# An output projection and a gate by seven products instead of eight, in a phase of their own

## The chip, the cores and the metric

The kernel runs on one core of one Trainium2 chip. The metric is the device time of one execution in microseconds; lower is better. All operands are float32. A matmul of float32 precision is made of three matmuls of a rounded type (float32r): each operand is split into a high half (the rounded value) and a low half (the rest), and high x high, low x high and high x low are added up in PSUM.

## The reference

A decoder trunk of two layers on 2048 tokens of 1024 features. Layer A is an mLSTM, layer B a dilated window attention. After each of them a gated embedding is added. What the change touches is the end of layer A:

```python
y = ht.reshape(Bsz, S, A_VW) * jax.nn.silu(z)          # 2048 x 1024
h = x + y @ w_out                                       # w_out 1024 x 1024
gate = jax.nn.sigmoid(rms_norm(h, norm_g) @ w_gate)     # w_gate 1024 x 1024
h = h + (p_l @ w_proj) * gate                           # p_l 2048 x 256
```

Layer B then reads h: it projects keys, values, queries and a gate from it, and adds to it.

## The kernel before, in words

Tokens go in NG = 4 groups of T = 512. Features lie on the 128 partitions, so an activation of one group is KD = 8 tiles of 128 x 512. A group passes through all of layer A and the projections of layer B before the next one starts: `a_in(g)` (mLSTM), `a_out(g)` (output projection and gate), `b_in(g)` (projections of layer B, written to DRAM). For the last group `b_in` runs beside the attention, whose small units are handed out one at a time by `pump()` between the steps of a projection.

`project` is the projection of everything: for each of the 8 slices of the contraction it loads a weight piece of 128 x 512 (`weights`: a DMA from SyncE's queue into `wraw`, then `split`: ScalarE writes the high half `wh`, VectorE subtracts it to get the low half `wl`), and makes 4 x 3 matmuls with 512 columns into 4 PSUM banks. There are 8 banks of 2 KB a partition in all, so one projection accumulates while the one before is read. The lines 145 and 147 are the matmuls with features and with tokens on the output's partitions.

In `a_out`, `mix_out` (L243) adds the banks to the residual x in SBUF, splits h times the norm's weight into the operands of the gate, and adds up its squares (`squares`: ScalarE squares, GpSimd adds, L184). `ple` multiplies the gate's banks by 1/rms of each token (`rstd_hooks`: a product with ones, GpSimd's power, a row spread by a product with a diagonal, L216), takes tanh, and multiplies by the embedding projection (`w_p`, contraction 256). `done` splits the new h for layer B, adds up squares, and writes it to DRAM (`h2d`, L519) for the residual of layer B. The mLSTM's result y is transposed on TensorE inside the output projection (`turn`), and goes from PSUM straight into operands.

The order of the instructions on each engine is written by a scheduler when the kernel is built, from program order and priorities: `tc.high_priority(offset=...)` moves what is in it ahead by so many places. On the chip each engine, and SyncE's DMA queue, runs its list in order and waits by semaphores. Tiles come from pools: a tag has a fixed number of buffers, and a new tile waits until the buffer's last reader is done.

Of the kernel before, what the change touches and what calls it, by code (L numbers as in the profile page):

```python
# [8 lines left out]
F32 = mybir.dt.float32  # L9
# [5 lines left out]
P = 128  # L15
SEQ = 2048
DM = 1024
T = 512
# [23 lines left out]
def trunk_kernel(ctx: ExitStack, tc: tile.TileContext, I: dict, O: dict, upto: int = 9):  # L42
# [6 lines left out]
    wp = ctx.enter_context(tc.tile_pool(name="wp", bufs=1))  # L49
    xp = ctx.enter_context(tc.tile_pool(name="xp", bufs=12))  # L50
    tm = ctx.enter_context(tc.tile_pool(name="tm", bufs=2))
    sm = ctx.enter_context(tc.tile_pool(name="sm", bufs=2))

# [28 lines left out]
    def scratch(name, shape):  # L82
        return O[name] if name in O else dram.tile(shape, F32, name=name)

    h2d = scratch("h2d", [NG, KD, P, T])
    kd = scratch("kd", [SEQ, 512])
# [82 lines left out]
    def sumsq(dst, src):  # L169
        jk = sm.tile([P, 512], BF16, name="jk", tag="jk", bufs=1)  # L170
        n = src.shape[-1]
        nc.scalar.activation(jk[:, :n], src, AF.Square, accum_out=dst)  # L172

    def pj(n=512):
        return sm.tile([P, n], F32, name="pj", tag="pj", bufs=8)

    def squares(acc, k, src, eng=nc.gpsimd):
        """acc += src**2 (acc = src**2 for k = 0)."""
        if k == 0:
            nc.scalar.activation(acc, src, AF.Square)  # L180
        else:
            sq = sm.tile([P, T], F32, name="sq", tag="sq", bufs=2)
            nc.scalar.activation(sq, src, AF.Square)  # L183
            eng.tensor_tensor(acc, acc, sq, op=ALU.add)  # L184

    def new_acc():
        return sm.tile([P, T], F32, name="acc", tag="acc", bufs=2)

    def token_rstd(acc):
# [4 lines left out]
        r = sm.tile([P, NT], F32, name="rst", tag="rst", bufs=4)  # L194
        rsqrt(r, ps[:, 0:NT], 1.0 / DM, NT)
        return r

    def spread(rst):
        """Diagonals of rst, [P, NT, P], in two parts."""
        rh = sm.tile([P, NT], F32R, name="rh", tag="rh", bufs=2)  # L200
        rl = sm.tile([P, NT], F32, name="rl", tag="rl", bufs=2)
        nc.vector.tensor_copy(rh, rst)
        nc.vector.tensor_tensor(rl, rst, rh.bitcast(F32), op=ALU.subtract)
        parts = []
        for r in (rh.bitcast(F32), rl):
            dg = sm.tile([P, NT, P], F32R, name="dg", tag="sq", bufs=2)
            nc.vector.tensor_tensor(dg, ident.unsqueeze(1).broadcast_to([P, NT, P]),
                                    r.unsqueeze(2).broadcast_to([P, NT, P]), op=ALU.mult)
            parts.append(dg)
        return parts  # L210

    def row_rstd(parts):
        """The same along the free axis on every partition: [P, T]."""
        ps = bank()
        for j, dg in enumerate(parts):
            nc.tensor.matmul(ps, onesr, dg.rearrange("p t s -> p (t s)"), start=j == 0, stop=j == 1)  # L216
        rb = sm.tile([P, T], F32, name="rb", tag="rb", bufs=1)
        nc.scalar.copy(rb, ps)
        return rb
# [8 lines left out]
    def tok(g):  # L228
        return slice(g * T, (g + 1) * T)

    def mix_out(src, nk, X, res, l, order=None, hooks={}):
        """h = res + X @ w (features on partitions), the operands of the gate and the sum of squares."""
        h = tm.tile([P, KD, T], F32, name="h", tag="v", bufs=1)
        for k in range(KD):
            nc.sync.dma_start(h[:, k], res[k])
        sq = new_acc()
        X2 = []
        for grp in range(2):
            acc = project(src[grp], 512, nk, X, True, order=order, hooks=hooks if grp == 0 else {})
            with tc.high_priority(offset=EVAC):  # L240
                for i in range(NT):
                    k = grp * NT + i
                    nc.vector.tensor_tensor(h[:, k], acc[i], h[:, k], op=ALU.add)  # L243
# [42 lines left out]
    def a_in(g):  # L286
# [13 lines left out]
        hooks = rstd_hooks(st, sq, *((R3, R4) if g else (5, 7)))  # L300
# [79 lines left out]
        Y = {}  # L380

        def turn(*ks):
            transposed([z[:, t] for t in range(NT)], ks, gam[:, G_H], Y)

# [4 lines left out]
        return Y, turn  # L389
# [24 lines left out]
    def mlstm_pre(pre, qk, t, n, ga):  # L414
        """What chunk n needs that does not depend on the state; ga: [P, 8] its gates."""
# [93 lines left out]
    def a_out(g, X, turn):  # L509
        hooks = {s: lambda k=k: turn(*k) for s, k in HO.items()}  # L510
        h, X, sq = mix_out(I["w_out_a"], 8, X, I["xT"][g], 0, (0, 1, 6, 7, 2, 3, 4, 5), hooks)
        sq2 = new_acc()
        X2 = []

        def done(k, hk):
            X2.append(new_x())
            split(*X2[k], hk, 1.0)
            squares(sq2, k, hk)
            nc.sync.dma_start(h2d[g, k], hk)  # L519

        ple(0, g, h, X, sq, done)
        return X2, sq2

    def rope_table(g, t, which):
        """[P, 2, 2, 64]: (g1 cos, g2 cos), (-g2 sin, g1 sin)."""
        n = g * NT + t
        cst = sm.tile([P, P], F32, name="cst", tag="cst", bufs=2)
        nc.sync.dma_start(cst, I["cs"][n * P:(n + 1) * P, :])
        tab = sm.tile([P, 2, 2, 64], F32, name="tab", tag=f"tab{which}", bufs=NT)
# [8 lines left out]
    def b_in(g, X, sq, late=lambda: None):  # L538
# [27 lines left out]
        st = {}  # L566
        acc = project(I["w_kv"][0], 512, 8, X, False, gam[:, G_KV], hooks={5: lambda: st.update(r=token_rstd(sq))})
        rst = st["r"]
# [39 lines left out]
    bp = ctx.enter_context(tc.tile_pool(name="bp", bufs=2))  # L608
# [17 lines left out]
    def attend(grp, r, res, b, kv, prev, finish, mdtag="md"):  # L626
        """One block of 128 queries of a head group with its own keys and those of the block before."""
# [159 lines left out]

    held = [[] for _ in range(NT)]
# [7 lines left out]
    b_in(NG - 1, X, sq, lambda: side.append(staged(first[-NL:] + tailed())))  # L796
# [25 lines left out]
def layout(inputs):  # L822
# [13 lines left out]

    wa = f["w_in_a"][0]
# [5 lines left out]
    d["w_out_a"] = pieces(f["w_out_a"][0], 512)  # L843
# [39 lines left out]
```

## Time and profile before

| | us |
|---|---|
| median of three runs | 2370.97 (2367.55 to 2373.04) |
| span of the profiled execution | 2372.5 |
| TensorE (PE) busy | 2318.8 (98%) |
| VectorE (DVE) busy | 1553.0 (65%) |
| ScalarE (ACT) busy | 1132.0 (48%) |
| GpSimd (POOL) busy | 605.1 (26%) |
| DMA | 330.86 MB, mean 139 GB/s |
| one `a_out` of 512 tokens (window 216.5 to 319) | 102.5 |

The profile is of one execution; its span is 1.5 us above the median of the runs. PEld is the loading of weights into TensorE, beside the matmuls. A line of the groups reads: source line, engine, operation, output tile <- input tiles, shapes, count, then busy time, mean duration in ns, idle time of the engine just before it and who ended that. An answer for one line of the source gives minimum, median and maximum of the durations instead. In a table of windows each engine has its busy time and number of instructions in that stretch.

### The profile page before, as it was taken

Reading aid. Unit: us, or ns where it says so; the run is one execution under the profiler, and the core shown is the slowest. Engines: PE = TensorE matmul, PEld = TensorE weight load, DVE = VectorE, ACT = ScalarE, POOL = GpSimd, SP = SyncE. Lnnn points to the kernel's source line nnn. Section 1 sums busy time; section 2 is a strip of 40 time slices with the busy share of each in tenths; the row PEclk is TensorE's granted clock in tenths of the full one; section 3 lists DMA queues with packets and bytes.
Section 4 is the critical chain, followed back from the end, with each engine's and each line's share of the span. In section 5 each row is a group of like instructions: output and inputs, shape, how many; then the busy total and the mean of one; then the engine's idle time right before and its main releaser. Section 6 shows DMA issues by size and latency. Waiting matters only on the chain.

```text
span 2372.5 us, 35281 instructions
## 1 busy us (share of the span) xinstructions
PE 2318.8 (98%) x11736; PEld 1976.7 (83%) x11736; DVE 1553.0 (65%) x3405; ACT 1132.0 (48%) x2730; POOL 605.1 (26%) x719
## 2 busy tenths in 40 slices
PE   8999999899999999999999999999999998999998
PEld 7889888788988887889888788888898887888887
DVE  7746675675567566746674676476754667786865
ACT  5334444543344454434444543344664665453643
POOL 5020244701212464011225710212112121220311
PEclk9999999999999999999999999999999999999999
DMA  5323334533234444323344443254563776464452
GB/s 157 125 75 121 111 122 158 164 101 120 66 125 124 149 137 142 118 90 114 99 129 152 145 125 120 66 165 124 196 222 126 233 239 217 145 195 159 146 164 94
DMA packets 186791, 330.86 MB, mean 139 GB/s; under 512 B 21168, under 2 KB 37872, under 8 KB 186608
## 3 DMA queue, kind: packets, MB, share of 16 engines
q1 hardware_dynamic: 186608, 328.59, 43.5%
q8 instruction: 93, 1.52, 0.3%
q14 instruction: 90, 0.74, 0.1%
HBM read 277.98 MB, written 50.53 MB: 138 GB/s over the span
## 4 chain that ended last, share of the span: by engine, by line
PE 84%; DVE 5%; POOL 4%; DMA 3%; issue 2%; ACT 1%; SPq 0%; DVEq 0%; POOLq 0%; ACTq 0%
PE bank L147 40%; PE bank L145 32%; PE bank L683 2%; PE bank L652 2%; PE bank L621 1%; PE bank L483 1%; PE bank L485 1%; PE bank L482 1%; POOL acc L184 1%; PE bank L160 1%; PE bank L672 1%; POOL rq L560 1%; DMA oo<-o2d 1%; PE bank L469 1%; DVE y L735 1%
## 5 line engine op out<-in xcount | busy, mean ns | idle before, releaser
L147 PE MATMUL bank<-wh,xh 128*128 128x512 f32 (+1 forms) x1664 | 641.4, 385 | 0.0
L147 PE MATMUL bank<-wh,xl 128*128 128x512 f32 (+1 forms) x1664 | 621.8, 374 | 0.0
L147 PE MATMUL bank<-wl,xh 128*128 128x512 f32 (+1 forms) x1664 | 621.0, 373 | 0.0
L95 ACT ACTIVATE wh<-wraw 128x512 fp32r<-128x512 f32 (+1 forms) x544 | 327.3, 603 | 579.8 <-PE bank L145 301.7
L97 DVE TENSOR_TENSOR wl<-wraw,wh 128x512 fp32r<-128x512 f32 (+1 forms) x512 | 361.1, 709 | 314.3 <-ACT wh L95 312.5
L145 PE MATMUL bank<-xh,wh 128*128 128x512 f32 x1280 | 508.9, 398 | 14.7 <-ACT wh L95 13.8
L145 PE MATMUL bank<-xh,wl 128*128 128x512 f32 x1280 | 503.4, 393 | 1.8 <-DVE wl L97 1.8
L145 PE MATMUL bank<-xl,wh 128*128 128x512 f32 x1280 | 501.7, 392 | 0.0
L147 PEld LDWEIGHTS bank<-wh,xl 128*128 128x128 f32 x1664 | 312.7, 188 | 50.5
L147 PEld LDWEIGHTS bank<-wh,xh 128*128 128x128 f32 x1664 | 313.1, 188 | 48.1
L147 PEld LDWEIGHTS bank<-wl,xh 128*128 128x128 f32 x1664 | 313.3, 188 | 47.7
L184 POOL TENSOR_TENSOR acc<-acc,sq 128x512 f32<-128x512 f32 x105 | 164.2, 1564 | 543.1 <-ACT sq L183 540.2
L145 PEld LDWEIGHTS bank<-xh,wh 128*128 128x128 f32 x1280 | 242.5, 190 | 65.1 <-ACT wh L95 15.0
L145 PEld LDWEIGHTS bank<-xh,wl 128*128 128x128 f32 x1280 | 243.2, 190 | 51.9 <-DVE wl L97 3.6
L145 PEld LDWEIGHTS bank<-xl,wh 128*128 128x128 f32 x1280 | 242.7, 190 | 51.5
L99 DVE SCALAR_TENSOR_TENSOR wl<-wraw,gam,wh 128x512 fp32r<-128x512 f32 x192 | 159.4, 830 | 156.4 <-ACT wh L95 155.2
L95 ACT ACTIVATE wh<-wraw,gam 128x512 fp32r<-128x512 f32 x192 | 138.4, 723 | 220.0 <-PE bank L147 166.2
L664 ACT ACTIVATE pr<-pr,nm 128x256 f32<-128x256 f32 (+1 forms) x192 | 86.5, 453 | 43.8 <-DVE nm L661 43.6
L558 POOL TENSOR_SCALAR ssb<-ssb,r 128x4 f32<-128x4 f32 x64 | 27.5, 430 | 257.0 <-ACT jk L172 235.5
L652 PE MATMUL bank<-kT,qT 128*128 128x128 f32 x600 | 79.2, 280 | 7.3 <-DVE pT L676 3.7
L652 PEld LDWEIGHTS bank<-kT,qT 128*128 128x128 f32 x600 | 73.8, 194 | 10.6 <-DVE pT L676 5.2
L560 POOL TENSOR_TENSOR rq<-ssb,mhalf 128x4 f32<-128x4 f32 x64 | 77.7, 1214 | 5.3
(402 smaller groups left out, 2943.6 us busy)
## 6 DMA issues: line engine op xcount, KB each, us to landing
wraw<-in_w_pg SPq DMA_DIRECT2D x128, 256.0 KB, 2.7
wraw<-in_w_in_b SPq DMA_DIRECT2D x128, 256.0 KB, 2.7
wraw<-in_w_z SPq DMA_DIRECT2D x96, 172.0 KB, 2.3
wraw<-in_w_v SPq DMA_DIRECT2D x64, 256.0 KB, 2.6
wraw<-in_w_o SPq DMA_DIRECT2D x64, 256.0 KB, 2.6
wraw<-in_w_out_a SPq DMA_DIRECT2D x64, 256.0 KB, 2.6
wraw<-in_w_kv SPq DMA_DIRECT2D x64, 256.0 KB, 2.7
kr<-kd SPq DMA_DIRECT2D x53, 256.0 KB, 4.0
```

Source lines behind the costliest of these rows:

```text
L95: nc.scalar.mul(dst_h, src, scale)
L97: nc.vector.tensor_tensor(dst_l, src, dst_h.bitcast(F32), op=ALU.subtract)
L99: nc.vector.scalar_tensor_tensor(dst_l, src, scale, dst_h.bitcast(F32), op0=ALU.mult, op1=ALU.subtract)
L145: nc.tensor.matmul(acc[i], w[:, cs], x, start=first, stop=last)
L147: nc.tensor.matmul(acc[i][:, :n], x[:, cs], w, start=first, stop=last)
L160: nc.tensor.transpose(tp[:, t * P:(t + 1) * P], tiles[t][:, k * P:(k + 1) * P], ident)
L184: eng.tensor_tensor(acc, acc, sq, op=ALU.add)
L558: nc.gpsimd.tensor_scalar(ss, ss, r2[:, t:t + 1], EPS, op0=ALU.mult, op1=ALU.add)
L560: nc.gpsimd.tensor_tensor(rq, ss, mhalf, op=ALU.pow)
L652: nc.tensor.matmul(sp[:, hh * n + j * P:hh * n + (j + 1) * P], qT[:, hs], kvs[j]["k"][:, hs], start=True, stop=True)
L664: nc.scalar.activation(pr[:, hh, :n], pr[:, hh, :n], AF.Exp, bias=nm[:, h:h + 1], accum_out=md[:, 4 + h:5 + h])
L683: nc.tensor.matmul(op[:, hs], pTs[h // 2][:, c0 + j * P:c0 + (j + 1) * P], kvs[j]["v"][:, hs], start=j == 0, stop=j == nk - 1)
```

## The change

Output projection and gate leave the loop over groups. The program has three phases now. The first runs `a_in` for all groups and writes y (transposed and scaled) to DRAM (`yd`), then the embedding projections of all groups (`ple_parts`, result in `pwd`). The second is new: four stages (output of tokens 0 to 1023, of 1024 to 2047, gate of the same two), each by Strassen's algorithm in its variant of Winograd. The 1024 tokens, the contraction and a block of 512 output columns are halved, and seven products of 512 tokens x 512 x 256 take the place of eight. Their operands are quarters of X and W or sums of such, split into halves after the sum; some results are carried on in PSUM (`chain`), some copied to SBUF and added there. Output goes to DRAM (`h1d`, then `h2d`). The third phase is layer B, which loads h from `h2d` and splits it. SBUF is laid out anew for each phase, in the same place; a tile of the new phase waits only for those tiles whose place it takes.

The products of a stage run in the order PR for each of two column blocks (nb). The operands of the next product's weights are made one product ahead; the seven operands of X of the next stage during the last column block of the stage before it.

```diff
-    for g in range(NG - 1):
-        b_in(g, *a_out(g, *a_in(g)))
-    X, sq = a_out(NG - 1, *a_in(NG - 1))
-    pa.close()
+    late = {}
+    for g in range(NG):
+        turn = a_in(g, late)
+        late = {s: lambda k=k, turn=turn: turn(*k) for s, k in HO.items()}
+    rest = list(late.values())
+    for g in range(NG):
+        ple_parts(g, ...)
+    pa.close()
+    p1.close()
...
         def turn(*ks):
-            transposed([z[:, t] for t in range(NT)], ks, gam[:, G_H], Y)
+            for k in ks:
+                tp = bank()
+                for t in range(NT):
+                    nc.tensor.transpose(tp[:, t * P:(t + 1) * P], z[:, t, k * P:(k + 1) * P], ident)
+                b = pj()
+                nc.scalar.mul(b, tp, gam[:, G_H, k:k + 1])
+                nc.sync.dma_start(yd[g, k], b)
...
+    PR = (1, 2, 6, 5, 7, 3, 4)
+    def sub(out, a, b, eng):
+        eng.tensor_tensor(out, a, b, op=ALU.subtract)
+    def halves(hi, lo, t):
+        nc.scalar.copy(hi, t)
+        nc.vector.tensor_tensor(lo, t, hi.bitcast(F32), op=ALU.subtract)
+    def x_operand(st, p):
+        hi = xs.tile([P, 4, T], F32R, name=f"xh{p}", tag=f"xh{p}")
+        lo = xs.tile([P, 4, T], F32R, name=f"xl{p}", tag=f"xl{p}")
+        st.X[p] = (hi, lo)
+        for kh in range(2):
+            ks = slice(2 * kh, 2 * kh + 2)
+            def ld(h, kq):
+                t = so.tile([P, 2, T], F32, name="xr", tag="xr", bufs=5)
+                k0 = 4 * kq + 2 * kh
+                nc.sync.dma_start(t, st.src[2 * st.s + h, k0:k0 + 2].rearrange("k p t -> p k t"))
+                return t
...
+            elif p == 6:
+                t, u, v = ld(1, 0), ld(1, 1), ld(0, 0)
+                nc.gpsimd.tensor_tensor(t, t, u, op=ALU.add)
+                sub(t, t, v, nc.vector)
+            elif p == 5:
+                t, u = ld(1, 0), ld(1, 1)
+                nc.gpsimd.tensor_tensor(t, t, u, op=ALU.add)
+            elif p == 7:
+                t, u = ld(0, 0), ld(1, 0)
+                sub(t, t, u, nc.gpsimd)
+            else:
+                t = ld(0, 1)
+                sub(t, t, st.X[6][0][:, ks].bitcast(F32), nc.vector)
+                sub(t, t, st.X[6][1][:, ks].bitcast(F32), nc.vector)
+            halves(hi[:, ks], lo[:, ks], t)
+    def w_load(st, nb):
+        B = {}
+        for kq, nq in ((0, 0), (1, 0), (0, 1), (1, 1)):
+            t = so.tile([P, 4, 256], F32, name="wr", tag="wr", bufs=5)
+            nc.sync.dma_start(t, st.w[nb, kq, nq].rearrange("p (k c) -> p k c", k=4))
+            if st.g is not None:
+                for k in range(4):
+                    nc.vector.tensor_scalar(t[:, k], t[:, k], gam[:, st.g, ...], None, op0=ALU.mult)
+            B[kq, nq] = t
+        return B
+    def w_operand(B, p):
...
+        elif p == 6:
+            t1 = B[0, 0]
+            sub(t1, B[0, 1], t1, nc.gpsimd)
+            t = B["t2"] = so.tile([P, 4, 256], F32, name="t2", tag="t2", bufs=1)
+            sub(t, B[1, 1], t1, nc.vector)
...
+        elif p == 7:
+            t = B[0, 1]
+            sub(t, B[1, 1], t, nc.gpsimd)
...
+        else:
+            t = B[1, 0]
+            sub(t, t, B["t2"], nc.gpsimd)
+        hi = so.tile([P, 4, 256], F32R, name="sh", tag="sh", bufs=2)
+        lo = so.tile([P, 4, 256], F32R, name="sl", tag="sl", bufs=2)
+        halves(hi, lo, t)
+    def multiply(st, p, w, banks, first, last):
+        for f in range(2):
+            for k in range(4):
+                for j, (a, b) in enumerate(((wh, xh), (wl, xh), (wh, xl))):
+                    nc.tensor.matmul(banks[f], a[:, k, cs], b[:, k], ...)
+    def run_stages(stages, hooks):
...
+        for p in PR:
+            x_operand(stages[0], p)
+            if p == 1:
+                fetch(0)
+        for n, (i, nb, p) in enumerate(flat):
+            with tc.high_priority(offset=60):
+                fetch(n + 1)
...
+            multiply(st, p, ops.pop(n), dst, p in (1, 2, 5), p in (4, 2, 3))
+            if nb == st.nbs - 1 and i + 1 < len(stages):
+                with tc.high_priority(offset=60):
+                    x_operand(stages[i + 1], p)
+            with tc.high_priority(offset=EVAC):
+                for j in range(2):
+                    if p in (1, 6, 5):
+                        parts[p, j] = st.first(h, f, dst[j])
+                    else:
+                        part = {2: 1, 7: 5, 3: 6, 4: None}[p]
+                        st.final(h, f, dst[j], parts.pop((part, j)) if part else None)
+    def gather(accs, h, v):
...
+            nc.scalar.activation(sqt, v, AF.Square)
+            nc.gpsimd.tensor_tensor(accs[h], accs[h], sqt, op=ALU.add)
+    def out_stage(s, accs):
+        def first(h, f, acc):
+            t = residual(h, f)
+            nc.vector.tensor_tensor(t, acc, t, op=ALU.add)
+            return t
+        def final(h, f, acc, t):
+            if t is None:
+                t = residual(h, f)
+            nc.vector.tensor_tensor(t, acc, t, op=ALU.add)
+            nc.sync.dma_start(h1d[2 * s + h, f], t)
+            gather(accs, h, t)
+    def ple_stage(s, rbs, accs):
+        def first(h, f, acc):
+            t = stile()
+            nc.scalar.copy(t, acc)
+            return t
+        def final(h, f, acc, t):
+            hh, pw = (so.tile([P, T], F32, name=n, tag=n, bufs=2) for n in ("hh", "pw"))
+            nc.sync.dma_start(hh, h1d[2 * s + h, f])
+            nc.sync.dma_start(pw, pwd[2 * s + h, f])
+            if t is None:
+                t = stile()
+                nc.vector.tensor_tensor(t, acc, rbs[h], op=ALU.mult)
+            else:
+                nc.vector.tensor_tensor(t, acc, t, op=ALU.add)
+                nc.gpsimd.tensor_tensor(t, t, rbs[h], op=ALU.mult)
+            nc.scalar.activation(t, t, AF.Tanh, scale=0.5)
+            nc.vector.scalar_tensor_tensor(t, t, 1.0, pw, op0=ALU.add, op1=ALU.mult)
+            nc.gpsimd.tensor_tensor(t, t, hh, op=ALU.add)
+            nc.sync.dma_start(h2d[2 * s + h, f], t)
+            gather(accs, h, t)
...
-    def b_in(g, X, sq, late=lambda: None):
+    def b_in(g, late=lambda: None):
+        X = []
+        for k in range(KD):
+            with tc.high_priority(offset=PRE):
+                raw = raw_piece(h2d[g, k], T)
+                X.append(new_x())
+                split(*X[k], raw, 1.0)
...
+    for g in range(NG - 1):
+        b_in(g)
```

More of the change, by code (lines that the diff above doesn't have):

```diff
@@ L226, in rstd_hooks, with both @@
         return {k0: first, k1: lambda: st.update(rb=row_rstd(st["d"]))}
-    def tok(g):
-        return slice(g * T, (g + 1) * T)
+    def both(*dicts):
+        out = {}
+        for d in dicts:
+            for s, f in d.items():
+                out.setdefault(s, []).append(f)
+        return {s: lambda fs=fs: [f() for f in fs] for s, fs in out.items()}
     def mix_out(src, nk, X, res, l, order=None, hooks={}):
@@ L299, in a_in @@
         st = {}
-        hooks = rstd_hooks(st, sq, *((R3, R4) if g else (5, 7)))
+        hooks = both(rstd_hooks(st, sq, *((R3, R4) if g else (5, 7))), late)
         qk = ap.tile([P, 2 * NH, T], F32, name="qk", tag="qk", bufs=1)
@@ L507, in mlstm, with ple_parts @@
             yield
[L509 to L522, printed above, removed]
+    def ple_parts(g, hooks):
+        pT = []
+        for k in range(2):
+            with tc.high_priority(offset=PRE):
+                praw = raw_piece(I["pT"][0, g, k], T)
+                pT.append(new_x())
+                split(*pT[k], praw, 1.0)
+        for grp in range(2):
+            acc = project(I["w_p"][0, grp], 512, 2, pT, True, 0.5, hooks=hooks[grp] if hooks else {})
+            with tc.high_priority(offset=EVAC):
+                for i in range(NT):
+                    b = pj()
+                    (nc.scalar.copy if i % 2 else nc.vector.tensor_copy)(b, acc[i])
+                    nc.sync.dma_start(pwd[g, grp * NT + i], b)
@@ new lines, in stile @@
+    def stile():
+        return so.tile([P, T], F32, name="st", tag="st", bufs=7)
+    def multiply(st, p, w, banks, first, last):
+        xh, xl = st.X[p]
+        wh, wl = w
+        for f in range(2):
+            cs = slice(f * P, (f + 1) * P)
+            for k in range(4):
+                for j, (a, b) in enumerate(((wh, xh), (wl, xh), (wh, xl))):
+                    nc.tensor.matmul(banks[f], a[:, k, cs], b[:, k], start=first and k == 0 and j == 0,
+                                     stop=last and k == 3 and j == 2, skip_group_check=True)
@@ new lines, in trunk_kernel, with row_hooks, cols, row @@
+    sq1, sq2, rb1 = [{}, {}], [{}, {}], [{}, {}]
+    rstb = {}
+    def row_hooks(s):
+        st = [{}, {}]
+        def cols():
+            for h in range(2):
+                st[h] = token_rstd(sq1[s][h])
+        def row(h):
+            parts = []
+            rh = sm.tile([P, NT], F32R, name="rh", tag="rh", bufs=2)
+            rl = sm.tile([P, NT], F32, name="rl", tag="rl", bufs=2)
+            nc.vector.tensor_copy(rh, st[h])
+            nc.vector.tensor_tensor(rl, st[h], rh.bitcast(F32), op=ALU.subtract)
+            for r in (rh.bitcast(F32), rl):
+                dg = so.tile([P, NT, P], F32R, name="dg2", tag="dg2", bufs=2)
+                nc.vector.tensor_tensor(dg, ident.unsqueeze(1).broadcast_to([P, NT, P]),
+                                        r.unsqueeze(2).broadcast_to([P, NT, P]), op=ALU.mult)
+                parts.append(dg)
+            return parts
+        def spread0(h):
+            st[h] = row(h)
+        def rows(h):
+            ps = bank()
+            for j, dg in enumerate(st[h]):
+                nc.tensor.matmul(ps, onesr, dg.rearrange("p t s -> p (t s)"), start=j == 0, stop=j == 1)
+            rb = so.tile([P, T], F32, name="rb2", tag="rb2", bufs=3)
+            nc.scalar.copy(rb, ps)
+            rb1[s][h] = rb
+        return [cols, lambda: spread0(0), lambda: (rows(0), spread0(1)), lambda: rows(1)]
@@ L524, in rope_table, with column @@
+    def column(s, h):
+        rstb[2 * s + h] = token_rstd(sq2[s][h], "rstb")
+    hk = {}
+    for i, s in ((1, 0), (2, 1)):
+        for p, f in zip((2, 5, 7, 3), row_hooks(s)):
+            hk[i, 0, p] = (f,)
+    hk[3, 0, 5] = (lambda: column(0, 0), lambda: column(0, 1))
+    run_stages([out_stage(0, sq1[0]), out_stage(1, sq1[1]),
+                ple_stage(0, rb1[0], sq2[0]), ple_stage(1, rb1[1], sq2[1])], hk)
+    column(1, 0)
+    column(1, 1)
+    p2.close()
     def rope_table(g, t, which):
@@ L794, in tailed @@
         return group2() + group1((3,), {}) + last + group0(1)
-    b_in(NG - 1, X, sq, lambda: side.append(staged(first[-NL:] + tailed())))
+    b_in(NG - 1, lambda: side.append(staged(first[-NL:] + tailed())))
     def turn(g, X, k):
```

120 lines of the change are left out of this document (98 added, 22 removed).

## The prediction

> **What bounds the kernel now.** I read the first two parts of the page (busy time by engine, then the span in slices), then the groups of instructions, then a table by stage, and last the timeline inside one stage.
>
> ```profile
> span 2372.5 us, 35281 instructions
> PE 2318.8 (98%) x11736; PEld 1976.7 (83%) x11736; DVE 1553.0 (65%) x3405; ACT 1132.0 (48%) x2730; POOL 605.1 (26%) x719
> PEclk9999999999999999999999999999999999999999
> PE 84%; DVE 5%; POOL 4%; DMA 3%; issue 2%; ACT 1%; SPq 0%; DVEq 0%; POOLq 0%; ACTq 0%
> ```
>
> The page says that TensorE sets the pace: busy 98%, 84% of the chain that ended last, at nearly the full granted clock. A matmul there seems to last 373 to 398 ns, but its end is modelled and matmuls overlap. What one costs is the distance between two starts, and that is in the timeline of PE in the first output stage:
>
> ```profile
> start us, us, engine line op out<-in xcount [idle before <-releaser]
> 283.64 0.39 PE L145 MATMUL bank<-xh,wh 128*128 128x512 f32 x1
> 283.88 0.40 PE L145 MATMUL bank<-xh,wl 128*128 128x512 f32 x1
> ...
> 318.80 0.39 PE L145 MATMUL bank<-xl,wh 128*128 128x512 f32 x1
> ```
>
> First and last of 156 starts in a row: 35.16 us / 155 = 0.227 us each, not 0.39. The saving must be priced at 0.227. The four stages that the change replaces (output projection, gate, embedding projection of one group of 512 tokens), by window:
>
> ```profile
> core 0: us, PE busy (x) PEld busy (x) DVE busy (x) ACT busy (x) POOL busy (x), PEclk, DMA share, GB/s
> 216.50:319.00 102.50, 102.50 (x469) 84.77 (x468) 68.12 (x101) 46.99 (x81) 17.82 (x12) 1.00 0.39 126
> 666.50:769.00 102.50, 102.50 (x469) 84.76 (x468) 68.13 (x101) 46.99 (x81) 17.84 (x12) 1.00 0.40 125
> 1116.50:1219.00 102.50, 102.50 (x469) 84.77 (x468) 68.14 (x101) 47.01 (x81) 17.86 (x12) 1.00 0.40 126
> 1567.00:1669.40 102.40, 102.40 (x469) 84.72 (x468) 68.11 (x101) 47.03 (x82) 17.87 (x12) 1.00 0.48 151
> 450.30:505.00 54.70, 47.85 (x204) 38.28 (x203) 34.52 (x54) 26.08 (x57) 20.09 (x32) 0.97 0.43 137
> 1669.40:1980.00 310.60, 293.73 (x1957) 264.11 (x1956) 193.73 (x671) 193.15 (x624) 58.10 (x72) 0.99 0.65 212
> ```
>
> Each stage holds 432 projection matmuls, 97.9 of its 102.5 us, and nobody is waited for. VectorE has 34 us to spare in it, GpSimd 85. Those spares are what the new phase spends.
>
> **TensorE's part.** Output and gate are 4 x 384 = 1536 matmuls now; by seven products they are 4 stages x 2 column blocks x 7 x 24 = 1344. 192 fewer at 0.227 us: 43.5 us saved, 1.8%. One product is 24 x 0.227 = 5.44 us, a block of seven ("slot" below) 38.1 us, the phase 304.7 us. The same work now: 1536 x 0.227 = 348.2, with four norm statistics (a ones product and a row of the norm, about 1.4 us of pitches each) 354 us. The embedding projection (48 matmuls a group) and the transposes of y move to the first phase at the same price.
>
> **The other engines' part.** Seven products need operands that are sums, each split in two halves again. I count what x_operand, w_operand, first, final and gather issue, priced from these rows (the first line names the columns; L548 is from the groups: busy, mean ns):
>
> ```profile
> engine op xcount: duration ns min/median/max, first and last start us, forms
> L97 DVE TENSOR_TENSOR wl<-wraw,wh x512: 500/686/1793, 7.6 to 2348.2; 128x512 fp32r<-128x512 f32 x140, 128x344 fp32r<-128x344 f32 x31
> L99 DVE SCALAR_TENSOR_TENSOR wl<-wraw,gam,wh x192: 732/752/1787, 309.2 to 1920.0; 128x512 fp32r<-128x512 f32 x192
> L243 DVE TENSOR_TENSOR h<-bank,h x64: 673/681/693, 240.2 to 2315.8; 128x512 f32<-128x512 f32 x64
> L548 DVE TENSOR_TENSOR pj<-bank,tab 128x256 f32<-128x256 f32 x128 | 52.9, 416 | 23.1 <-PE bank L147 23.1
> L184 POOL TENSOR_TENSOR acc<-acc,sq x105: 1267/1622/2313, 243.9 to 2319.3; 128x512 f32<-128x512 f32 x105
> L533 POOL TENSOR_TENSOR tab<-qkg,cst x64: 315/758/837, 9.2 to 1355.0; 128x64 f32<-128x64 f32 x64
> L503 DVE TENSOR_SCALAR o<-o,rr x64: 345/349/355, 154.5 to 1570.5; 128x256 f32<-128x256 f32 x64
> L95 ACT ACTIVATE wh<-wraw x544: 472/631/654, 6.8 to 2352.9; 128x512 fp32r<-128x512 f32 x154, 128x344 fp32r<-128x344 f32 x28
> ```
>
> The new tiles have 1024 elements a partition, which no row shows. VectorE: 256 to 512 elements go from 416 to 686 ns, so 686 + 2 x 270 = 1.22 us (upper bound twice 686, 1.37). GpSimd: 64 to 512 go from 315 to 1267, so 1267 + 512 x 2.125 = 2.36 us (upper bound 2.53). I take the slopes. GpSimd at 512: 1.28 (near the minimum).
>
> - X set of a stage: VectorE 14 lower halves and 6 subtractions, 20 x 1.22 = 24.4; GpSimd 6 x 2.36 = 14.2. It is made in the last slot of the stage before; the first in its own first slot.
> - W of a slot: VectorE 7 halves and 1 subtraction, 9.8; GpSimd 3 x 2.36 = 7.1.
> - Out slot, besides: 14 PSUM adds on VectorE, 9.5; gather on GpSimd 7 x 1.28 = 9.0.
> - Gate slot, besides: VectorE 8 PSUM adds or multiplies 5.4, 8 scalar_tensor_tensor 6.0, gamma scaling 16 x 0.35 = 5.6; GpSimd 6 multiplies by the norm, 8 adds of h1, 7 of gather, 21 x 1.28 = 26.9.
> - ScalarE: 14 copies for X and 7 for W at about 1.0 us, with squares and tanh some 30 us in the fullest slot of 38: hidden.
>
> Side by side, the fullest slot (gate, with the next X set) has 51 us of VectorE and 48 of GpSimd against 38.1 of TensorE, the others less. That alone would leave little of the 43.5 us. But they don't run side by side. The maxima above (1793 where 686 is usual, 2313 where 1267 is least) come from moments like this, SBUF operands on both engines:
>
> ```profile
> 298.65 1.82 POOL L184 TENSOR_TENSOR acc<-acc,sq 128x512 f32<-128x512 f32 x1 [2.48 <-ACT sq L183]
> 299.23 1.79 DVE L97 TENSOR_TENSOR wl<-wraw,wh 128x512 fp32r<-128x512 f32 x1
> 300.64 1.52 POOL L184 TENSOR_TENSOR acc<-acc,sq 128x512 f32<-128x512 f32 x1 [0.17 <-ACT sq L183]
> 300.94 1.78 DVE L97 TENSOR_TENSOR xl<-h,xh 128x512 fp32r<-128x512 f32 x1
> ```
>
> From 298.65 to 302.72 two GpSimd adds and two VectorE subtractions ended: 2 x 1.28 + 2 x 0.69 = 3.94 us of work in 4.07 us. They took turns. The PSUM adds (L243) never exceed 693 ns: with one operand in PSUM there is no such wait. So I add the two engines' SBUF-only work into one account.
>
> The account: X set 24.4 + 14.2 = 38.6; out slot 9.8 + 7.1 + 9.0 = 25.9; gate slot 9.8 + 7.1 + 6.0 + 26.9 = 49.8. Slot by slot, the larger of account and TensorE:
> - out, tokens 0 to 1023: 25.9 + 38.6 = 64.5 (own X), 64.5 (next X)
> - out, 1024 to 2047: 38.1 (TensorE), 64.5
> - gate, 0 to 1023: 49.8, 88.4
> - gate, 1024 to 2047: 49.8, 49.8
>
> Sum 469 us. If late X work slides into the one slot with room, 457. The gamma scaling (64 x 0.35 = 22.4) is left out, as no row shows it beside a large GpSimd instruction; with it 492 at most. The Trainium skill, SBUF — State Buffer, section "Who interferes with whom", describes the turn-taking as an exclusive lock held for the whole instruction, which this trace bears out (1.79 us against 0.69), and counts tensor_scalar in its faster mode among what is locked out, which no row here shows; by it the sum below would be 2514.
>
> Ahead of the phase PE waits for the first X and W: a load (3), two copies (2), a half (1.2), about 6 us (0 if tiles come free early, 12 if loads of 512 KB land slowly). Behind it the key/value weights go into SBUF that the seventh product still reads: 4 us (1 to 8), the wait that 450.30 now shows. Phase: 469 + 10 - 354 = +125.
>
> **Waits and queues.** VectorE is in order: behind a half that waits for GpSimd stand the PSUM adds and the next product's W halves. An accumulator must be read before the product after next adds into it, 5.44 us of cover, which one GpSimd instruction of 2.36 us and two halves use up; so the wait reaches PE. SyncE: 376 transfers come for 192 that go; by L519's row an issue takes
>
> ```profile
> L519 SPq DMA_DIRECT2D h2d<-h x32: 319/327/682, 292.5 to 1679.7; - x32
> h<-h2d SPq DMA_DIRECT2D x32, 256.0 KB, 4.7
> ```
>
> so 184 x 0.33 = 61 us of SyncE, spread over the program and off the path. hh and pw have two buffers: a pair of finals needs a landing (4.7), 0.75 and two GpSimd adds, about 8 us, 32 per slot; covered by the 49.8, and were that cover gone, by TensorE's 38.1. Bytes in the phase: 88 X and 32 W loads of 512 KB and 160 transfers of 256 KB, 105 MB; in 479 us that is 219 GB/s, near the 212 of the window 1669 to 1980 (share 0.65). In 305 us it would be 344, above the 326 that 212 / 0.65 gives: memory too speaks against a phase at TensorE's pace.
>
> **First and last phase.** The embedding projections, alone, move 3.5 MB per 10.9 us, 321 GB/s, at that ceiling: +5 (0 to 16). Now, entering q from a late layer-B projection costs: the window from 450.30 has 54.7 us for 192 matmuls and statistics worth 44.8, three times, 30 us in all, mostly GpSimd's squares behind the rope work. Without that neighbour I credit half, -15 (0 to -30). Between layer-B groups operands must be split from memory: +6 (0 to 9). Together -4.
>
> **Sum.** 2372.5 + 125 - 4 = 2493.5 by the profiled span. The median of the runs is 1.5 us below it: 2492 us.
>
> **The rivals.**
> 1. *VectorE and GpSimd hardly meet, so the phase is faster.* Then each slot is the largest of the three engines alone: 43.7 + 43.7 + 38.1 + 43.7 + 38.1 + 51.2 + 38.1 + 38.1 = 335; 335 + 10 - 354 - 4 = -13: 2358, down to 2328 if only TensorE counts. For it: in 102.5 us of a present stage GpSimd's 17.8 hurts nobody. Against: in the new phase the two have 200 us (VectorE) and 257 us (GpSimd) of SBUF-only work, and VectorE 82 besides. It decides below a phase of 358 us, that is if less than a sixth of the 134 us between 335 and 469 is paid.
> 2. *Half is paid*, since chains leave the engines idle at different moments: 402 + 10 - 354 - 4, 2425.
> 3. *TensorE's clock falls in the gaps.* After waits of 2.75 and 0.71 us the pitch doubles for some matmuls:
>
> ```profile
> 473.36 0.79 PE L216 MATMUL bank<-dg,onesr 128*128 128x512 f32 x1 [0.71 <-DVE dg L207]
> 473.95 0.63 PE L145 MATMUL bank<-xh,wh 128*128 128x512 f32 x1
> 474.38 0.63 PE L145 MATMUL bank<-xh,wl 128*128 128x512 f32 x1
> ```
>
> At 0.427 throughout, a slot is 71.7: three out slots gain 7.2, three gate slots 21.9, +87: 2579. Against: the five or so slow matmuls after one gap are 1 us, which a slot bound by the account hides. The Trainium skill, TensorE: Matmul & The Clock Gate, Part 1, asks for an idle window of about 3.4 us; by it only the slots with 64.5 and 88.4 (gaps of 3.8 and 7.2 us a product) would be touched, where it is hidden.
>
> **How the numbers follow.** Taking turns 0.60 (own range 2455 to 2530: 457 to 492, and the small terms' bounds), half paid 0.13, slow clock or worse queues 0.09, rival 1 0.18, of which 0.03 near zero. 0.2% is about what a measurement of this kernel can tell from no change. Faster 0.15, same 0.03, slower 0.82. Range 2400 to 2575: it leaves out rival 1 and the far end, 0.2 together.
>
> **What would show it.** Right: in the phase between mLSTM and layer B PE busy near two thirds, subtractions of 1024 elements on VectorE averaging well over 1.22 us and GpSimd's over 2.36, PE waiting for the lower half of W and X, the gate slots of tokens 0 to 1023 longest. Wrong: a phase under 360 us with PE above 90%; means at the bare durations; or the loss lying at the borders of the phase.

## The result, and the profile after

| | before | after |
|---|---|---|
| median of four runs each, same chip, us | 2371.73 (2367.55 to 2373.04) | 2541.11 (2539.20 to 2542.09) |
| span of the profiled execution, us | 2372.5 | 2540.3 |

The ratio is 1.0707 (95% interval 1.069 to 1.0725): 7.1% slower. The forecast was slower, 2492 us with a range of 2400 to 2575; the time is 49 us above the point and inside the range.

The page after, its busy times, three of its rows of 40 slices and the chain that ended last by engine (its shares add up to 48%: it is followed back over about half the span only, so they say little of the new phase):

```profile
span 2540.3 us, 35469 instructions
PE 2335.1 (92%) x11544; PEld 1973.5 (78%) x11544; DVE 1708.7 (67%) x3429; ACT 1171.7 (46%) x2722; POOL 824.4 (32%) x823
...
PE   8999999999999968697767599999999998999999
...
POOL 1022013002202034555777546473720310211211
PEclk9999999999999988898878799999999999999999
...
PE 37%; POOL 3%; DVE 3%; DMA 2%; issue 2%; ACT 1%; SPq 0%; DVEq 0%; POOLq 0%; ACTq 0%
```

TensorE runs 192 matmuls fewer, yet its share fell from 98% to 92%. The hole is in slices 15 to 23, where PE's digits are 5 to 9, its clock's 7 to 9 and GpSimd's 3 to 7: the new phase (a slice is 63.5 us). Outside it TensorE is nearly as full as before (97% busy in the first phase and in layer B). The table by stage gives each part its time (rows: first phase's `a_in`, embedding projections, the seven-product phase, its border to layer B, layer B; columns as in the prediction's table):

```profile
0.00:868.50 868.50, 845.04 (x4255) 731.51 (x4256) 570.37 (x1313) 382.20 (x821) 151.19 (x190) 0.99 0.35 109
868.50:919.80 51.30, 46.97 (x221) 38.36 (x219) 28.50 (x51) 27.57 (x49) 0.89 (x1) 1.00 0.89 306
919.80:1414.00 494.20, 370.13 (x1400) 288.71 (x1400) 387.87 (x348) 175.82 (x226) 312.75 (x158) 0.86 0.61 204
1414.00:1443.90 29.90, 3.88 (x17) 3.56 (x16) 11.13 (x16) 9.94 (x17) 20.36 (x31) 0.54 0.54 178
1443.90:2540.30 1096.40, 1069.07 (x5656) 911.32 (x5656) 710.86 (x1704) 576.16 (x1612) 339.24 (x444) 0.99 0.55 177
```

Set against the prediction's terms (before: 865.6 for the four `a_in`, 409.9 for the four replaced windows, 1097.0 for layer B):

| part, us | predicted | measured |
|---|---|---|
| four `a_in`, with the transposes moved in | 863 | 868.5 |
| embedding projections alone | 48.5 | 48.0 (868.5 to the last one at 916.5) |
| second phase: start, products, border | 6 + 469 + 4 = 479 | 3.3 + 494.2 + 29.9 = 527.4 |
| layer B | 1103 | 1096.4 |
| sum | 2493.5 | 2540.3 |

So the whole error of 47 us lies in one row. Inside the phase TensorE's 494.2 us split as follows. Its waits from 919 to 1414 add up to 126.9 us, of which 2.9 lie just ahead of the first product and 124 inside the phase. The four longest entries of the list of waits of PE (total, times, longest):

```profile
PE bank L660 <- DVE sl L577: 55.7, 23, 13.7
PE bank L660 <- ACT sqt L711: 17.4, 2, 10.6
PE bank L660 <- ACT xh L576: 15.0, 3, 11.7
PE bank L660 <- ACT sh L576: 14.3, 7, 5.8
```

The 1344 matmuls are worth 305 us at 0.227. Of the 65 us left, some 54 are slow ones: 275 starts came over 0.3 us after the one before (waits taken out), at about 0.2 us extra each. The rest is norm statistics.

Three groups tell what the two elementwise engines were doing, with busy time, mean ns, idle time before; below them the answers for three lines, with minimum, median and maximum in ns:

```profile
L577 DVE TENSOR_TENSOR xl<-xr,xh 128x1024 fp32r<-128x1024 f32 x56 | 106.9, 1921 | 24.4 <-ACT xh L576 24.2
L577 DVE TENSOR_TENSOR sl<-wr,sh 128x1024 fp32r<-128x1024 f32 x47 | 81.3, 1730 | 17.9 <-ACT sh L576 15.1 <-issue 2.8
L621 DVE TENSOR_SCALAR wr<-wr,gam 128x256 f32<-128x256 f32 x64 | 46.3, 770 | 1.9 <-DMA wr<-in_s_pg 1.9
...
L577 DVE TENSOR_TENSOR xl<-xr,xh x56: 1207/1353/3425, 919.9 to 1314.5; 128x1024 fp32r<-128x1024 f32 x56
L621 DVE TENSOR_SCALAR wr<-wr,gam x64: 335/346/2486, 1105.8 to 1355.6; 128x256 f32<-128x256 f32 x64
L604 POOL TENSOR_TENSOR xr<-xr x8: 2348/2588/2970, 946.6 to 1274.2; 128x1024 f32<-128x1024 f32 x8
```

The minima are the bare prices that the prediction estimated (1.207 us for its 1.22 on VectorE, 2.348 for its 2.36 on GpSimd); the means are longer, by 43 and 59% for VectorE's two kinds of lower halves and by 26% for GpSimd's 48 sums of 1024 elements (2.96 us). The longest wait shows how that reaches TensorE (timeline of VectorE, GpSimd and PE):

```profile
1298.12 3.41 DVE L577 TENSOR_TENSOR xl<-xr,xh 128x1024 fp32r<-128x1024 f32 x2
1298.27 2.18 POOL L752 TENSOR_TENSOR st<-st,hh 128x512 f32<-128x512 f32 x1 [5.17 <-DVE st L751]
...
1301.45 5.28 DVE L621 TENSOR_SCALAR wr<-wr,gam 128x256 f32<-128x256 f32 x8
1303.67 2.39 POOL L573 TENSOR_TENSOR wr<-wr 128x1024 f32<-128x1024 f32 x1 [1.02 <-DVE wr L621]
...
1306.65 1.21 DVE L577 TENSOR_TENSOR sl<-wr,sh 128x1024 fp32r<-128x1024 f32 x1
...
1307.92 0.80 PE L660 MATMUL bank<-xh,sl 128*128 128x512 f32 x1 [13.69 <-DVE sl L577]
```

VectorE finishes operands of X that came late for the stage that has already begun, scales eight blocks of W (5.28 us for 8 x 0.35 = 2.8, with GpSimd at work beside it for most of that time) and only then makes the half of W that product 2 needs. TensorE stood for 13.7 us.

### The profile page after: what moved, and what is told of

The parts are those of the page before. It is cut to its first block, busy times and chain, and to the rows that moved or that the text cites. A ratio compares the mean times of both kernels' runs of the same rounds, so it can differ in the third digit from the quotient of the medians.

```text
span 2540.3 us, 35469 instructions
## 1 busy us (share of the span) xinstructions
PE 2335.1 (92%) x11544; PEld 1973.5 (78%) x11544; DVE 1708.7 (67%) x3429; ACT 1171.7 (46%) x2722; POOL 824.4 (32%) x823
## 5 line engine op out<-in xcount | busy, mean ns | idle before, releaser
L108 DVE TENSOR_TENSOR wl<-wraw,wh 128x512 fp32r<-128x512 f32 (+1 forms) x384 | 256.3, 669 | 229.2 <-ACT wh L106 228.3
L156 PE MATMUL bank<-xh,wh 128*128 128x512 f32 x768 | 305.5, 398 | 7.4 <-ACT wh L106 7.0
L156 PE MATMUL bank<-xh,wl 128*128 128x512 f32 x768 | 300.0, 391 | 0.0
L156 PE MATMUL bank<-xl,wh 128*128 128x512 f32 x768 | 299.8, 391 | 0.0
L660 PE MATMUL bank<-xh,sh 128*128 128x512 f32 x448 | 192.5, 431 | 57.2 <-ACT sqt L711 17.4
L660 PE MATMUL bank<-xh,sl 128*128 128x512 f32 x448 | 193.9, 433 | 55.7 <-DVE sl L577 55.7
L660 PE MATMUL bank<-xl,sh 128*128 128x512 f32 x448 | 191.3, 427 | 4.6 <-DVE xl L577 4.6
L156 PEld LDWEIGHTS bank<-xh,wh 128*128 128x128 f32 x768 | 144.6, 188 | 35.7 <-ACT wh L106 7.0
L156 PEld LDWEIGHTS bank<-xl,wh 128*128 128x128 f32 x768 | 144.4, 188 | 30.7
L156 PEld LDWEIGHTS bank<-xh,wl 128*128 128x128 f32 x768 | 144.8, 189 | 29.1 <-DVE wl L108 0.8
```

The costliest lines, as they stand in the source:

```text
L108: nc.vector.tensor_tensor(dst_l, src, dst_h.bitcast(F32), op=ALU.subtract)
L156: nc.tensor.matmul(acc[i], w[:, cs], x, start=first, stop=last)
L660: nc.tensor.matmul(banks[f], a[:, k, cs], b[:, k], start=first and k == 0 and j == 0, stop=last and k == 3 and j == 2, skip_group_check=True)
```

## The experiments

Two theories of the phase. **A**: the sums of VectorE and GpSimd take turns, so their times add. **B**: the loss would be there without turns, from queues in a fixed order, chains of sum, copy and half, and loads. Three of the border (last product to layer B's first matmul): **P**, the table loads `cst` hold SyncE's queue; **Q**, the norm sums (`column`) hold layer B; **R**, the last outputs' own chain, store and reload. Where a term is compared between kernels below, it is the window of the phase in each kernel's own trace. Each run is one execution; the four of the changed kernel above lie within 3 us.

**1. The GpSimd instructions of the phase on VectorE.** Nothing else changes; 160 instructions move (48 sums of operands, 56 of gather, 56 of the gate's outputs).

```diff
-                nc.gpsimd.tensor_tensor(t, t, u, op=ALU.add)
+                nc.vector.tensor_tensor(t, t, u, op=ALU.add)
 ... and so in x_operand, w_operand, gather and final
```

> All additions, subtractions and multiplications that GpSimd makes in the new phase (48 of 1024 elements, 110 of 512) go to VectorE; GpSimd keeps only the norm's power. Theory A (VectorE and GpSimd take turns on SBUF operands, so their times add up): VectorE's own work rises from 281 to 281 + 48 x 1.21 + 110 x 0.68 = 414 us, but nobody blocks it; slot by slot, with TensorE's 38.1 as the least, 425, with the present share of other waits 435 to 450 against 494, and the tail behind the phase falls from 30 to some 20: total 2475 to 2495; VectorE's subtractions of 1024 elements at 1.21 us mean. Theory B (the phase is long because VectorE is slow and its list in the wrong order, GpSimd only helps it): the instructions keep their present means (1.9 and 1.2 us), VectorE gets over 200 us more, total over 2600.

2447.58 us (before on that chip: 2375.93). Products 410.1 us for 494.2, border 22.5 for 29.9:

```profile
918.80:1328.90 410.10, 342.50 (x1400) 271.46 (x1400) 376.62 (x504) 179.54 (x229) 9.10 (x6) 0.91 0.73 247
```
```profile
L577 DVE TENSOR_TENSOR xl<-xr,xh x56: 1209/1216/1226, 919.0 to 1250.7; 128x1024 fp32r<-128x1024 f32 x56
L621 DVE TENSOR_SCALAR wr<-wr,gam x64: 337/346/353, 1073.0 to 1285.9; 128x256 f32<-128x256 f32 x64
```

VectorE ran 504 instructions for 348 and was busy 11 us *less*. The spread of its durations is gone: nothing longer than 1226 where 3425 occurred. Here an engine that works in parallel was worse than none. B's forecast of over 2600 falls, and the phase is shorter even than A's 435 to 450, whose sum of bare times was too long for one engine: its busy time came to 377 us for the 414 forecast.

**2. GpSimd instructions that read one operand.** In place of each two-operand instruction of GpSimd stands a scaling by one of the same tile; the sums that GpSimd made are left out.

```diff
+    def alone(out, a):
+        nc.gpsimd.tensor_scalar(out, a, 1.0, None, op0=ALU.mult)
...
-                nc.gpsimd.tensor_tensor(t, t, u, op=ALU.add)
+                alone(t, t)
```

> Each two-operand GpSimd instruction of the phase becomes a GpSimd tensor_scalar (times 1) that reads one of its operands and writes the same tile: all the sums on GpSimd are left out, all its dependencies, queue places and transfers stay. By the row of the existing one-operand instruction (1.49 us for 512 elements) GpSimd gets slower, about 303 us of own work for 254. Theory A, in the form that two-operand instructions on both sides are needed (the one-operand row of the kernel before hardly delayed VectorE: 0.99 us at most): phase 345 to 390 for 494, total 2390 to 2440, VectorE at 1.21 us. Theory A in the form of the Trainium skill (any GpSimd instruction that reads SBUF excludes a two-operand VectorE one): the account grows from 471 to about 520, total 2560 to 2600. Theory B (GpSimd's length and the order of the queues): also longer than now, 2560 or more, but with VectorE's instructions near 1.21 us.

2500.88 us (2375.93), products 448.5. VectorE's halves of X:

```profile
L580 DVE TENSOR_TENSOR xl<-xr,xh x56: 1209/1225/2057, 919.5 to 1269.0; 128x1024 fp32r<-128x1024 f32 x56
```

Mean 1345 for 1921: one-operand work on GpSimd delays VectorE a little, and seldom. But the replacement is itself slower (1490 ns median at 512 elements, where the two-operand form has a minimum of 1260), so GpSimd's own work grew, and the two effects are mixed. None of the three expectations was met; run 8 repeats it at equal time. The Trainium skill, SBUF — State Buffer, "Who interferes with whom", lets any GpSimd instruction that reads SBUF shut out a VectorE instruction with two SBUF inputs; for one operand that is not what the 1225 median shows.

**3. The next stage's X without its priority.**

```diff
-                with tc.high_priority(offset=60):
-                    x_operand(stages[i + 1], p)
+                x_operand(stages[i + 1], p)
```

> The operands of X for the next stage lose their priority of 60 places, so that they stand behind the weights' operands and the reads of PSUM in the lists. Theory A: the account of 471 us stays, so the phase stays within 20 us of 494, the waits only move: total 2520 to 2560. Theory B: the 56 us that TensorE waits for lower halves of weights come from X work ahead of them in VectorE's list; most of it goes, total 2480 to 2500.

2536.41 us (2375.93), products 481.7 for 494.2, as A expected. This order of the list is worth 12.5 us, not the loss.

**4. The same phase with eight products.** Everything passes through DRAM as in the change, but X and W are split as they come, and the eight plain products need no sums. Besides, fewer halves have to be made (of 4 operands of X a stage and 4 of W a column block, where it was 7 and 7), and the operands of W have four buffers where they had two.

```diff
-                sub(t, t, u, nc.gpsimd)          # and all other sums of x_operand, w_operand
...
-        flat = [... for p in PR]                 # seven products
+        flat = [... for nq in range(2) for h in range(2) for kq in range(2)]   # eight
```

> The same separate phase over 1024 tokens, passed through DRAM, with the same tiles and the same queues, but eight plain products of quarters accumulated in PSUM instead of seven of sums. TensorE 8 x 8 x 5.44 = 348 us. Theory A: X set 8 x 1.21, W slot 4 x 1.21, no sums; account 14 to 45 us a slot against 43.5 of TensorE: phase 355 to 375, border up to 30, total 2395 to 2430. Theory C (the passage through DRAM and the separate phase cost the time, not the sums): the phase is about as long as now or, with 43.5 us more on TensorE, longer: 2520 or more.

2401.60 us (2375.93): products 357.8, border 21.3, and a wait of 9.6 us ahead.

```profile
928.10:1285.90 357.80, 357.76 (x1592) 296.27 (x1593) 181.90 (x246) 118.77 (x158) 121.47 (x91) 0.99 0.60 203
```

TensorE is full (357.76 of 357.80) at a clock of 0.99. That is A's forecast, and C falls. The separate phase through DRAM costs 1.1% by itself, at its edges; inside, with GpSimd busy for a third of the time, it costs nothing. With seven products TensorE had 192 matmuls fewer and took 136 us longer.

**5, 6, 7. The border.** Eight buffers for `cst` (P), the norm sums after layer B's first group (Q), and both.

```diff
-        cst = bg.tile([P, P], F32, name="cst", tag="cst", bufs=2)
+        cst = bg.tile([P, P], F32, name="cst", tag="cst", bufs=8)
```
```diff
-    column(1, 0)
-    column(1, 1)
     p2.close()
...
         b_in(g)
+        if g == 0:
+            column(1, 0)
+            column(1, 1)
```

> The 30 us between the last product and the first matmul of layer B. One change: the tile of the rope table's loads (cst) gets 8 buffers for 2, so that its loads on SyncE no longer wait for GpSimd. Theory P (SyncE is in order, and the loads of h stand behind the cst loads that wait for GpSimd's rope work at 1432): the loads of h go out at about 1415, the border falls from 30 to 12 to 18 us, total 2522 to 2530. Theory Q (the loads of h wait for the last TensorE instruction of the phase, the sums of the norm, which wait for GpSimd's last addition): the border stays at 30, total 2540.

> The two last sums of the norm (column(1, 0) and column(1, 1)) are called behind the first group of layer B, which doesn't need them; their accumulators move to a pool that outlives the phase. Theory Q: no TensorE instruction of the phase is behind the last product, so the loads of h go out at 1414 to 1418 and the border falls to 12 to 18 us, total 2522 to 2530. Theory P: the loads still stand behind the cst loads, the border stays near 30, total about 2540.

> Both changes. P or Q alone: as the one that helped. If each alone leaves 30 us because the two waits end at the same time: 12 to 18 us only here, total 2522 to 2530. Theory R (the border is the last outputs' own chain on GpSimd): 25 us or more even here.

2541.65, 2541.09 and 2540.96 us (before 2372.97 on their chip); border 28, 29 and 27.2 us. P and Q fall, alone and together. What is left is in SyncE's queue and TensorE's start, first of the changed kernel:

```profile
1428.12 0.32 SPq L753 DMA_DIRECT2D h2d<-st  x1
1429.23 3.03 SPq L812 DMA_DIRECT2D cst<-in_cs  x2
1432.35 6.67 SPq L115 DMA_DIRECT2D wraw<-h2d  x8
...
1443.93 0.80 PE L158 MATMUL bank<-wh,xh 128*128 128x512 f32 x1 [11.21 <-ACT wh L106]
```

The last store of h leaves 14 us after the last product; behind it in the same queue stand the loads with which layer B begins, and 11.6 us pass from the first load of h (1432.35) to the first matmul. With both edits the two pieces are 13.3 (to 1427.00) and 11.5 us (from 1429.34). That is R. Run 1, with the last outputs' additions off GpSimd, has a border of 22.5, which fits it. In no run do the loads stand ahead of the last store, so R is what remains, not what was taken away.

**8. As run 2, but over 27/32 of each tile**, so that GpSimd's own time is that of the changed kernel. Again the sums on GpSimd are left out.

```diff
+    def alone(out, a):
+        n = a.shape[-1] * 27 // 32
+        nc.gpsimd.tensor_scalar(out[..., :n], a[..., :n], 1.0, None, op0=ALU.mult)
```

> As the kernel with one-operand GpSimd instructions, which leaves out the sums on GpSimd, but each only over 27/32 of the tile, so that GpSimd's own time is that of the changed kernel (1.29 us for 1.27, 2.39 for 2.37; 254 us in all). The one thing that differs from the changed kernel is then that GpSimd reads one SBUF operand and not two. Theory A: what the phase loses against 494 us is the price of taking turns: phase 400 to 430, total 2445 to 2475. Theory B (GpSimd's length in the chain of each output is what counts): the phase stays above 470, total above 2510.

2478.42 us (2372.97), products 432.1 for 494.2.

```profile
921.20:1353.30 432.10, 356.83 (x1400) 281.89 (x1400) 284.23 (x348) 175.93 (x227) 286.33 (x158) 0.89 0.68 235
```
```profile
L581 DVE TENSOR_TENSOR xl<-xr,xh x56: 1208/1226/1926, 921.4 to 1262.9; 128x1024 fp32r<-128x1024 f32 x56
L625 DVE TENSOR_SCALAR wr<-wr,gam x64: 334/346/986, 1083.7 to 1299.1; 128x256 f32<-128x256 f32 x64
L577 POOL TENSOR_SCALAR sac<-sqt x56: 1286/1293/2158, 962.4 to 1366.1; 128x432 f32<-128x432 f32 x56
```

GpSimd has as many instructions (158) in the same places and queues, their least times no shorter than before (1286 for 1260); all but the norm's six now scale one operand over 27/32 of a tile, where they added or multiplied two over the whole. VectorE is busy 284 us for 388, and the phase is 62 us shorter. The smaller part of the tile isn't what relieves VectorE: in run 2, over whole tiles, it is busy 289. Products and total lie 2 and 3 us above A's ranges and far from B's. The replacement also no longer waits for its second operand to arrive, which the rows don't separate; but the 104 us are taken off VectorE's own instructions, which kept their operands. Some turns remain (986 and 1926 where 346 and 1226 are usual; GpSimd's 56 of gather go up to 2158 for 1293), which the 62 us don't count.

**9. Run 1, with gamma on ScalarE.**

```diff
-                    nc.vector.tensor_scalar(t[:, k], t[:, k], gam[...], None, op0=ALU.mult)
+                    nc.scalar.mul(t[:, k], t[:, k], gam[...])
```

> On top of the kernel with everything on VectorE (total 2447.6, phase 410): the 64 scalings of the gate's weights by gamma (22 us of VectorE) go to ScalarE, busy 180 of those 410 us. Theory A' (without GpSimd the phase is bound by VectorE, which is busy 377 of 410 us): phase 385 to 398, total 2422 to 2436. Theory D (the chain from a load over the halves to TensorE, with one product of lead, is what is left): within 5 us of 2447.

2437.13 us (2368.01), products 398.8 for run 1's 410.1: 1 us outside A', 10 below D's 2447.

**10. Run 9 without any sum of operands.** The 80 sums and differences of X and W are left out; seven products, their splitting, PSUM additions, loads and stores stay.

> On top of that, all 80 sums of 1024 elements that make the operands of X and W are left out (the seven products then multiply plain quarters); transfers, halves, products, outputs and gate stay. VectorE loses 97 us. Theory A': phase 310 to 335, total 2350 to 2375, so that the seven products pay only if their sums are nearly free. Theory D: the chain stays, phase above 360, total above 2400.

2390.13 us (2368.01), products 343.5:

```profile
920.90:1264.40 343.50, 322.25 (x1400) 262.99 (x1400) 272.15 (x360) 201.90 (x293) 7.70 (x6) 0.98 0.84 295
```

This lies between the two theories; 24 us of waits are left. With free sums Strassen beats eight products inside the phase by 14 us (357.8 to 343.5), a third of the 43.5, and the whole is still 0.9% slower than before. No version of these beats the kernel before.

The products, step by step (waits are TensorE's own, with the 2.6 to 2.9 us just ahead of the first product; slow is the number of starts over 0.3 us apart, waits taken out):

| kernel | products, us | waits, us | slow | total against before on its chip |
|---|---|---|---|---|
| eight products (4) | 357.8 | 9.6, ahead | 11 | 1.011 |
| seven, no sums (10) | 343.5 | 23.8 | 58 | 1.009 |
| sums on VectorE, gamma on ScalarE (9) | 398.8 | 60.6 | 147 | 1.029 |
| sums and gamma on VectorE (1) | 410.1 | 70.1 | 153 | 1.030 |
| GpSimd at equal time, one operand (8) | 432.1 | 77.8 | 207 | 1.044 |
| the change | 494.2 | 126.9 | 275 | 1.071 |

The 80 sums cost 55 us on VectorE alone, gamma 11, and giving those 160 instructions to GpSimd 84 more, of which run 8 takes 62 away again without making GpSimd's own time shorter. A is shown: the turns are worth more (84 in run 1, 62 in run 8) than all 80 sums or gamma. B is not nothing: in run 8 the phase is still 127 us above TensorE's 305, of which 75 are waits and about 41 (207 x 0.2) slow matmuls. How the 75 divide among the order of the queues, the chains and the loads stays open.

## Why the prediction was right or wrong

- **The bound and the saving: right.** Eight products kept TensorE full for 357.8 us, against the 354 priced at 0.227 a matmul.
- **Turns between VectorE and GpSimd: right in kind, shown by runs 1 and 8**, and the prices of 1024 elements were within 15 ns. The rival in which the two hardly meet (335) falls. But so does its size: run 8, where turns are few, took 432 and not 335; the slot model knew neither TensorE's waits nor its slow matmuls.
- **The account, 469: mis-sized by 25.** The term left out was gamma, with 22.4 named as its upper end, "as no row shows it beside a large GpSimd instruction". It stood there blocked, 770 ns on average for 346 alone. With it counted the prediction's own 492 is close to the measured 494. The Trainium skill, SBUF — State Buffer, "Who interferes with whom", says so of tensor_scalar, and this trace agrees (maximum 2486 in the change, 353 in run 1): its 2514 was the better figure for this term. That the sum comes so close is in part luck. It puts 157 us on turns (492 for 335); runs 1 and 8 show 84 and 62, and the 97 us by which run 8 exceeds 335 come from waits and slow matmuls, which the account doesn't hold.
- **The slots: wrong in detail.** Gate, tokens 0 to 1023, was to be longest with 88.4 in its second block. By slot (first and second column block of each stage in turn) the phase measured

```profile
919.80:994.20 74.40, 48.36 (x168) 36.13 (x169) 49.29 (x41) 23.61 (x26) 33.35 (x14) 0.79 0.81 278
994.20:1047.20 53.00, 44.34 (x169) 34.71 (x168) 48.55 (x32) 19.63 (x23) 38.69 (x16) 0.90 0.75 259
1047.20:1104.50 57.30, 44.50 (x189) 36.18 (x188) 42.14 (x42) 18.72 (x24) 24.65 (x13) 0.88 0.63 218
1104.50:1156.10 51.60, 42.76 (x170) 33.52 (x169) 47.72 (x36) 19.79 (x23) 38.06 (x16) 0.93 0.69 228
1156.10:1224.30 68.20, 50.73 (x190) 40.56 (x189) 59.71 (x72) 23.73 (x33) 37.96 (x23) 0.80 0.50 171
1224.30:1284.20 59.90, 45.50 (x169) 34.29 (x167) 48.79 (x35) 25.12 (x34) 48.48 (x24) 0.91 0.59 191
1284.20:1360.50 76.30, 49.77 (x184) 39.10 (x185) 64.32 (x67) 26.76 (x39) 51.75 (x31) 0.80 0.51 170
1360.50:1414.00 53.50, 44.17 (x169) 34.22 (x168) 27.35 (x25) 18.46 (x28) 39.80 (x25) 0.90 0.37 118
```

  and the block with 88.4 took 59.9. Late X work slides into the next stage's first block (57.3, 68.2 and 76.3, where 38.1, 49.8 and 49.8 were forecast), and in the last two of these product 2 waits longest. The prediction named the sliding, but only into the slot with room. An account adds up wherever its work is done, so the sum could come out near the mark with the slots wrong.
- **The border, 4: mis-sized by 26**, half of the error. It was priced as a wait for a place in SBUF. What ends it is another step: the last block's chain on GpSimd, ScalarE and VectorE, its store, and layer B's loads behind that store in one queue. A phase that ends in DRAM, with the next one beginning there, pays its drain and its fill in full; that even eight products paid 21.3 shows it isn't Strassen's.
- **The clock rival: dismissed for the wrong reason.** "Five or so slow matmuls after one gap" were 275 in the phase, about 54 us of TensorE's time (clock 0.86). Whether they cost time or lie under the account isn't separated: they vanish together with the gaps. The rival's own sum is also short: at 0.427 throughout, the slot with 38.1 would add another 33.6 us to its +87.
- **The point of no gain: a slip.** With 10 us for start and border and 4 gained outside, the products may take 348 us, not 358, before the change loses; that is a tenth of the 134 us, not a sixth. It touches neither the point nor the range.
- **Small terms.** Entering q takes 47.7 to 48.0 us where it took 54.7, and TensorE has no gap there now; the second group's:

```profile
222.80:270.50 47.70, 47.70 (x228) 39.70 (x227) 29.61 (x56) 20.20 (x36) 6.32 (x16) 1.00 0.37 110
```

  That is -21 in three places for the -15 credited; but the `a_in` as a whole came out 5.5 longer than forecast. Most of what was gained is given back by a new wait at the end of an mLSTM, where VectorE now splits the next group's X (total, times, longest):

```profile
PE bank L504 <- DVE cstate L505: 16.4, 4, 5.3
```

  The projections alone were right to 0.5 us (48.0, DMA share 0.89), and layer B gained 0.6 where 6 were charged.

By size: border +26, account +25, `a_in` +5.5, layer B -6.6, start -2.7, projections -0.5; together 47.

## What to carry to other kernels

Price the operands of a cheaper algorithm before its products: here each seven products saved 5.4 us of TensorE and needed elementwise work that, in the two engines' own times, exceeds the products (some 480 us by the account with gamma, for 305). Don't count VectorE and GpSimd as two engines when both read two SBUF tensors; add their times, tensor_scalar included, and try first whether one engine alone is faster, as it was here by 84 us. And give a phase that begins and ends in DRAM its drain and fill (21 to 30 us here) before anything it does inside.

## What the runs showed of the hardware that was not expected

**Slow matmuls follow short waits of TensorE, and late.** This is PE in the changed kernel; before 1353.56 it had run without a wait for over 5 us:

```profile
1351.25 0.39 PE L660 MATMUL bank<-xh,sh 128*128 128x512 f32 x1
1353.56 0.50 PE L660 MATMUL bank<-xh,sl 128*128 128x512 f32 x1 [1.93 <-DVE sl L577]
1353.90 0.39 PE L660 MATMUL bank<-xl,sh 128*128 128x512 f32 x1
...
1354.83 0.57 PE L660 MATMUL bank<-xh,sh 128*128 128x512 f32 x1
1355.19 0.63 PE L660 MATMUL bank<-xh,sl 128*128 128x512 f32 x1
...
1357.75 0.63 PE L660 MATMUL bank<-xh,sl 128*128 128x512 f32 x1
1358.18 0.45 PE L660 MATMUL bank<-xl,sh 128*128 128x512 f32 x1
1358.47 0.39 PE L660 MATMUL bank<-xh,sh 128*128 128x512 f32 x1
```

After a wait of 1.93 us it resumes at full pace, falls to about 0.43 us between starts 1.3 us later and recovers 3.4 us after that, with no further wait. So a gap of under 2 us is followed by eight slow matmuls, another 1.6 us lost (a second gap, of 1.81 us, ends at 1268.10 with the same picture), while the wait of 2.38 us that ends at 1345.90 costs next to nothing. That the gap is the cause is inferred from the order in time. The Trainium skill, TensorE: Matmul & The Clock Gate, Part 1, asks for an idle window of about 3.4 us; the slow stretch has that length here, but the idle time ahead of it was shorter.

**One operand or two.** A GpSimd instruction that reads one SBUF tensor left VectorE's median at 1225 ns, with single ones up to 2057; one that reads two brought it to 1353, with up to 3425. In run 8, 46 of VectorE's lower halves ran beside a GpSimd instruction for nearly all their time, and 33 of these took under 1.26 us; of 36 such in the changed kernel 5 did.
